# A transformer-like layer on one core: the down product of its channel mixer as seven half-size products

## The chip, the core and the metric

One core of a Trainium2 chip runs the whole program. TensorE multiplies, VectorE (DVE in the profile), ScalarE (ACT) and GpSimd (POOL) do the elementwise work, SyncE (SP) issues the transfers. The metric is the device time of one execution in microseconds; the median of three runs of the kernel before is 1348.81 us (1346.97 to 1351.1).

## The reference, cut to what matters

One layer of a streaming encoder over 592 tokens (16 meta, 512 prompt, 64 sample): a differential attention and a gated delta rule side by side, merged, and then the channel mixer, which works on the 576 tokens whose result is given back:

```python
x = x + mix @ p["w_out"]
h2 = _rmsnorm(x, p["norm2"])
x = x + jnp.square(jax.nn.relu(h2 @ p["w_up"])) @ p["w_down"]
```

`w_up` is 1024 x 4096, `w_down` 4096 x 1024, all in 32-bit floats. The change lies in the last line.

## The kernel before, in words

Every product is made of three: each operand is split into a high part (rounded to the type that TensorE multiplies in one pass, by a copy on ScalarE) and a low part (what is left, by a subtraction on DVE or GpSimd), and high x high, high x low and low x high are added up in PSUM. Tokens lie along the free axis, in two halves of 288.

`stream` (line 292) runs a list of tasks, one for each 256 columns of a weight matrix. While the body of task i issues matmuls, it hands out small steps at each `yield`, from the body's second on: the high part of the next weights' first 512 rows (`split_hi`, 128 x 1024 elements), their low part (`split_lo`), the same for the other 512 rows, and the loads for the task after next into the two buffers `wr0` and `wr4` (tiles `wr_*`, 512 KB each). High and low parts are the tiles `wh_*` and `wl_*`, two buffers each. `VG` (line 281) chooses DVE or GpSimd for a low part by the clocks that the planner `Pace` (line 52) keeps for each engine.

`feat` (line 362) is the body of most tasks: four parts (two blocks of 128 output features x two halves of tokens), each of 8 blocks of 128 input features x 3 matmuls, 24 in all, into one PSUM bank; it yields after every eight. The bank's evacuation `evac` is issued when its last matmul has been. Three banks go round (tag `pg`); the other five (tag `pt`) serve everything else.

The channel mixer: `up_task(i)` (line 1405), sixteen of them, each for 256 of the 4096 hidden features. Its evacuation of one part reads PSUM with relu and the norm's scale (DVE, tile `ur`), squares (ScalarE), and splits into `uh` (copy on ScalarE) and `ul` (subtraction on DVE). `down_tasks(qd)` (line 1421) are four tasks for each quarter of the hidden features; each multiplies 1024 hidden features into 256 outputs and adds the PSUM result to the running sum `x1` (DVE, tile `x`). The order is written out at line 1468: up 0 to 4, down 0, up 5 to 8, down 1, up 9 to 12, down 2, up 13 to 15, down 3. In the last quarter `write_y` (line 1437) turns each finished pair of blocks of `x1` and stores it.

Ahead of the mixer, `norm2_part` (line 1358) splits `x1` times the norm's weight into `h2h` and `h2l` and adds up squares; `token_norm` (line 1378) makes the reciprocal root for each token and spreads it over the partitions as `rstd2`, by a product of ones with five scaled identities `dg`. The up product starts on the unscaled values; only its evacuation needs `rstd2`.

Engines run their instructions in the order in which the program issues them, and wait on semaphores for each other. `Chain` objects (attention, norm, output) are woven in by `drive` (line 341).

Of the kernel before, what the change touches and what calls it, by code (L numbers as in the profile page):

```python
# [8 lines left out]
F32 = mybir.dt.float32  # L9
F32R = mybir.dt.float32r  # L10
# [7 lines left out]
P = 128  # L18
# [12 lines left out]
QHALVES = ((0, 288), (288, 576))  # L31
QTILES = [(0, 128), (128, 128), (256, 128), (384, 128), (512, 64)]
# [167 lines left out]
class Task:  # L200


    def __init__(self, nm, src, c0, body, need=None):
        self.nm, self.src, self.c0, self.body = nm, src, c0, body
        self.need = need or (lambda: True)


@with_exitstack
def stream_step_kernel(
# [24 lines left out]
    gp = Tags(pace, ctx.enter_context(pool("gates")), gth=3, st=3)  # L234
# [57 lines left out]
    def stream(tasks):  # L292
        raw, wts = {}, {}

        def load(i, k):
            if i < len(tasks) and tasks[i].src is not None:
                t = tasks[i]

                def go():
                    raw[i, k] = wp.tile([P, 4, 256], F32, name=f"wr_{t.nm}{k}", tag=f"wr{k}")  # L300
                    Q.dma_start(raw[i, k], t.src[k * P:(k + 4) * P, t.c0:t.c0 + 256].rearrange("(k p) n -> p k n", p=P))
                pace.stores.append((wp.when(f"wr{k}", 1), ((i, k),), go))
                if "start" not in done:
                    pace.flush(key=(i, k))

        def split_hi(i, k):
            pace.flush(key=(i, k))
            if (i, k) in raw:
                if k == 0:
                    wts[i] = [wp.tile([P, KC, 256], F32R, name=f"{x}_{tasks[i].nm}", tag=x) for x in ("wh", "wl")]  # L310
                S.copy(wts[i][0][:, k:k + 4], raw[i, k])

        def split_lo(i, k):
            if (i, k) in raw:
                hi, lo = (x[:, k:k + 4] for x in wts[i])
                (VG(2.1, 1024) if "start" in done else G).tensor_tensor(lo, raw.pop((i, k)), hi.bitcast(F32), ALU.subtract)

        for k in (0, 4):
            load(0, k)
        yield False  # L320
        for k in (0, 4):
            split_hi(0, k)
            split_lo(0, k)
        yield False
        for k in (0, 4):
            load(1, k)
        for i, t in enumerate(tasks):
            while not t.need():
                yield False
            ahead = deque()  # L330
            for f, j, k in ((split_hi, 1, 0), (split_lo, 1, 0), (split_hi, 1, 4), (load, 2, 0), (split_lo, 1, 4),
                            (split_lo, 1, 8), (load, 2, 4)):
                ahead.append(lambda f=f, j=j, k=k: f(i + j, k))
            for n, x in enumerate(t.body(wts.pop(i, None))):
                if n >= 1 and ahead and "start" in done and x is None:
                    ahead.popleft()()
                yield x is None
            while ahead:
                ahead.popleft()()
# [21 lines left out]

    def feat(xh, xl, nm, evac, m=P, ms=(0, P), halves=QHALVES, after="start", last=None):

        def body(w):
            parts, full = [(h, c) for h in range(len(ms)) for c in halves], deque()
# [23 lines left out]

    def tok(xh, xl, nm, evac):  # L390
# [16 lines left out]
    cst = cp.tile([P, 3 * P], F32, name="cst")  # L407
    ident = cst[:, 0:128]
    UP = (cst[:, 128:256], cst[:, 256:384])
    identr = cp.tile([P, P], F32R, name="identr")  # L410
    onesr = cp.tile([P, P], F32R, name="onesr")
    lowr = cp.tile([P, 2, P], F32R, name="lowr")
    nmr = cp.tile([P, 2, P], F32R, name="nmr")
    kn_bc = cp.tile([P, 64], F32, name="kn_bc")
# [3 lines left out]
    vec2 = cp.tile([P, 75], F32, name="vec2")  # L418
# [7 lines left out]
    g_t = cp.tile([P, NT, 8], F32, name="g_t")  # L426
    beta_t = cp.tile([P, NT, 8], F32, name="beta_t")
    gh_t = cp.tile([P, NT, 8], F32R, name="gh_t")
    gl_t = cp.tile([P, NT, 8], F32R, name="gl_t")
    kdec = cp.tile([P, NT, 8], F32, name="kdec")  # L430
    egl = cp.tile([P, NT + 1, 8], F32, name="egl")
    rn = cp.tile([P, 4, 2, NT, 4], F32, name="rn")
    cs_t = cp.tile([P, 2, 72], F32, name="cs_t")
# [32 lines left out]
    def begin(sp):  # L466
# [20 lines left out]
        Q.dma_start(cst[:, P:3 * P], consts[:, P:3 * P])  # L487
# [63 lines left out]
    def prepare(sp):  # L551
# [15 lines left out]
        V.tensor_scalar(nmr, cst[:, P:3 * P].rearrange("p (a b) -> p a b", a=2), -MASKED, MASKED, ALU.mult, ALU.add)  # L567
# [468 lines left out]
    def attn_tasks(p):  # L1036
        def evac(i):
            def f(t, n, ps):
                x = gp.tile([P, 256], F32, name=f"st{p}{i}{t}", tag="st")
# [3 lines left out]
                if i < 2:  # L1043
                    jk = gp.tile([P, 256], F32, name=f"sq{p}{i}{t}", tag="sq")
# [4 lines left out]
                if t == NT - 1:  # L1049
                    if i == 1:  # L1050
                        r = rn[:, p].rearrange("t i a m -> t (i a m)")
                        rsqrt(gp, r, 40, 1.0 / 64, EPS, tag="ar", out=r)
# [305 lines left out]
    def norm2_part(j):  # L1358
# [6 lines left out]
        if j == 0:  # L1365
            late["sq"] = rp.tile([P, TQ], F32, name="sqa", tag="sqa")
# [198 lines left out]
```

## Time and profile before

| | us |
|---|---|
| median of three runs | 1348.81 |
| profiled execution | 1348.32 |
| its span, first to last instruction | 1346.5 |
| TensorE matmul busy | 1297.8 |
| DVE busy | 694.0 |
| ScalarE busy | 564.5 |
| GpSimd busy | 264.7 |
| chain: four up tasks (384 matmuls) | 50.92 |
| chain: four down tasks (384 matmuls) | 50.97 |

Busy times are sums over instructions, in the profile as shares of the span. Matmuls are pipelined: each is printed with some 0.295 us though the next starts 0.13 us later, so times of TensorE are best read from starts. The same holds in small for the other engines: an instruction can start some 0.08 us ahead of the printed end of the one before. The chain of waits is followed back from the last instruction; its rows give a start, a length, an engine and a tile.

### The profile page before, as it was taken

The numbers are of one execution on the slowest core, as the hardware profiler recorded it, in microseconds if no ns is written. First come the engines' busy times: TensorE is split into PE (matmuls) and PEld (weight loads), VectorE is DVE, ScalarE is ACT, GpSimd is POOL, SyncE is SP. The second block draws the span as 40 slices with busy tenths as digits, with TensorE's granted clock in tenths as the row PEclk, the third lists the DMA queues.
The fourth block names the chain that finished last, engine by engine and source line by source line (L and its number), as shares of the span: only waits on it lengthen the run. The fifth ranks groups of instructions, "written<-read, shape, count | busy, mean of one in ns | idle before, by whom it ended". The sixth has DMA issues, their size and how long they took to land.

```text
span 1346.5 us, 25748 instructions
## 1 busy us (share of the span) xinstructions
PE 1297.8 (96%) x10365; PEld 1260.4 (94%) x10365; DVE 694.0 (52%) x1547; ACT 564.5 (42%) x1354; POOL 264.7 (20%) x283
## 2 busy tenths in 40 slices
PE   2999999999999999999899999999999999999998
PEld 2998899999899999998788899999999999999998
DVE  5766899533457624448877844445333233233232
ACT  3556544343563343346676723233431431431421
POOL 5101412200132000062524102100410410310300
PEclk9999999999999999999999899999999999999999
DMA  6313343532644422685644256622223223222231
GB/s 174 90 53 116 100 124 113 169 91 72 196 135 127 141 78 66 189 242 162 198 141 135 94 203 226 204 78 80 79 79 95 76 82 94 67 92 86 72 112 53
DMA packets 163947, 161.07 MB, mean 120 GB/s; under 512 B 23546, under 2 KB 143628, under 8 KB 163828
## 3 DMA queue, kind: packets, MB, share of 16 engines
q1 hardware_dynamic: 162372, 155.99, 38.2%
q0 software_dynamic: 1456, 3.44, 0.9%
q8 instruction: 81, 1.33, 0.4%
q14 instruction: 38, 0.31, 0.1%
HBM read 124.46 MB, written 37.88 MB: 121 GB/s over the span
## 4 chain that ended last, share of the span: by engine, by line
PE 46%; DVE 3%; DMA 1%; ACT 1%; issue 0%; SPq 0%; DVEq 0%; ACTq 0%
PE pg_dn L164 15%; PE pg_u L164 15%; PE pg_o L164 4%; PE pg_bb L164 4%; PE pg_ba L164 3%; PE pg_g L164 1%; DVE sc L164 1%; PE ppo L164 1%; DVE mx L164 1%; PE psc L164 1%; PE pwT L164 1%; ACT sc L164 0%; DMA thb<-th_d 0%; PE pxr L164 0%; PE pyo L164 0%
## 5 line engine op out<-in xcount | busy, mean ns | idle before, releaser
L164 PE MATMUL pg_dn<-uh,wh_dn 128*128 128x288 f32 x512 | 151.6, 296 | 0.0
L164 PE MATMUL pg_dn<-ul,wh_dn 128*128 128x288 f32 x512 | 151.6, 296 | 0.0
L164 PE MATMUL pg_u<-h2h,wh_u 128*128 128x288 f32 x512 | 151.4, 296 | 0.0
L164 PE MATMUL pg_u<-h2h,wl_u 128*128 128x288 f32 x512 | 151.2, 295 | 0.0
L164 PE MATMUL pg_u<-h2l,wh_u 128*128 128x288 f32 x512 | 151.2, 295 | 0.0
L164 PE MATMUL pg_dn<-uh,wl_dn 128*128 128x288 f32 x512 | 151.1, 295 | 0.0
L164 PE MATMUL pg_a<-wh_a,hh 128*128 128x256 f32 (+1 forms) x480 | 136.3, 284 | 2.0 <-ACT sq L164 2.0
L164 PE MATMUL pg_a<-wh_a,hl 128*128 128x256 f32 (+1 forms) x480 | 136.3, 284 | 0.0
L164 PE MATMUL pg_a<-wl_a,hh 128*128 128x256 f32 (+1 forms) x480 | 135.4, 282 | 0.0
L164 PE MATMUL pg_d<-hl,wh_d 128*128 128x336 f32 (+1 forms) x384 | 116.1, 302 | 0.6 <-DVE hl L164 0.6
L164 PE MATMUL pg_d<-hh,wh_d 128*128 128x336 f32 (+1 forms) x384 | 116.0, 302 | 0.6 <-ACT hh L164 0.6
L164 PE MATMUL pg_d<-hh,wl_d 128*128 128x336 f32 (+1 forms) x384 | 115.8, 302 | 0.0
L164 POOL TENSOR_TENSOR wl_u<-wr_u,wh_u 128x1024 fp32r<-128x1024 f32 x22 | 52.9, 2402 | 260.5 <-ACT wh_u L164 260.5
L164 DVE TENSOR_TENSOR x<-x,pg_dn 128x288 f32<-128x288 f32 x64 | 29.1, 454 | 132.5 <-PE pg_dn L164 132.5
L164 PEld LDWEIGHTS pg_u<-h2h,wh_u 128*128 128x128 f32 x512 | 96.5, 189 | 0.1
L164 PEld LDWEIGHTS pg_u<-h2l,wh_u 128*128 128x128 f32 x512 | 96.5, 189 | 0.0
L164 PEld LDWEIGHTS pg_u<-h2h,wl_u 128*128 128x128 f32 x512 | 96.4, 188 | 0.0
L164 PEld LDWEIGHTS pg_dn<-uh,wl_dn 128*128 128x128 f32 x512 | 96.3, 188 | 0.0
L164 PEld LDWEIGHTS pg_dn<-ul,wh_dn 128*128 128x128 f32 x512 | 96.1, 188 | 0.0
L164 PEld LDWEIGHTS pg_dn<-uh,wh_dn 128*128 128x128 f32 x512 | 96.1, 188 | 0.0
L164 PEld LDWEIGHTS pg_a<-wh_a,hh 128*128 128x128 f32 (+1 forms) x480 | 86.5, 180 | 3.1 <-ACT sq L164 2.5
L164 PEld LDWEIGHTS pg_a<-wh_a,hl 128*128 128x128 f32 (+1 forms) x480 | 86.7, 181 | 0.7 <-issue 0.6
(371 smaller groups left out, 3536.6 us busy)
## 6 DMA issues: line engine op xcount, KB each, us to landing
wr_u<-in_w_up_dram SPq DMA_DIRECT2D x32, 512.0 KB, 3.6
wr_dn<-in_w_down_dram SPq DMA_DIRECT2D x32, 512.0 KB, 3.5
wr_d<-in_w_in_dram SPq DMA_DIRECT2D x24, 512.0 KB, 3.9
wr_a<-in_w_in_dram SPq DMA_DIRECT2D x24, 512.0 KB, 4.1
wr_g<-in_w_in_dram SPq DMA_DIRECT2D x16, 512.0 KB, 5.5
at_d<-st SPq DMA_DIRECT2D x48, 128.0 KB, 2.2
th_d<-gt SPq DMA_DIRECT2D x16, 288.0 KB, 2.2
wr_z<-in_w_in_dram SPq DMA_DIRECT2D x8, 512.0 KB, 3.8
```

The costliest lines, as they stand in the source:

```text
L164: r = f(*a, **kw)
```

## The change

A down task takes four blocks of its factors as a 2 x 2 matrix: the weights as rows (even and odd blocks of 128 hidden features) by columns (two blocks of 128 outputs), the hidden values as rows by columns (two halves of tokens). Seven products of half the size replace the eight, after the scheme of Strassen and Winograd. Each is of 4 blocks of hidden features x 3 matmuls of 128 x 128 x 288.

The sums of the weights are made by four DVE steps (`s1` to `s4`, 128 x 512 elements each, partly in place); high and low parts are then made of 3.5 x 1024 elements in place of 2 x 1024, in two blocks of buffers, the second within the task itself. The seven combinations of hidden values are made by the up tasks' evacuation: a tile of seven for each up task, with four differences. Of the up task's two token halves, the second block of features takes the later one first (`turn`). The seven products go into four PSUM banks; three go on in a bank after DVE has read it. P1 and P6 are added into a tile `G` of their own over the four quarters, and `G` is added to three of the four result blocks in the last quarter. The first down task of the last quarter issues its products in the order `LATE`. The low parts of weights stay off GpSimd from the out product on (`VG` then gives DVE). Constants of the early stages move to a pool that is closed before the mixer, to make room; the weight loads have a third buffer `wrx`; `token_norm` multiplies with the reciprocal root spread by a stride of zero instead of the scaled identities; the squares go to `rstd2` and the `gth` buffers.

```diff
@@ VG
+        if "tail" in done:
+            return V
         return V if max(pace.t["DVE"], pace.t["PE"]) + 1.05 * n <= ...
@@ stream
+        users = {"wr0": deque(), "wr4": deque(), "wrx": deque()}
...
+        def room():
+            return len([x for x in held if not x["free"]]) < 2
...
+        def plain_steps(i):
...
+            return [(room, lambda: hi(0)), (None, lambda: lo(0)), (None, lambda: hi(1)), (None, lambda: load("wr0")),
+                    (None, lambda: lo(1)), (None, lambda: load("wr4"))]
...
+        def seven_steps(i):
...
+            def s1():
+                (_, a21), (_, a22) = quarters(0), quarters(1)
+                st["s"] = late["wx"].tile([P, 4, 256], F32, name=f"s_{tasks[i].nm}", tag="ws")
+                VG(2.1, 512).tensor_tensor(st["s"][:, :, 0:128], a21, a22, ALU.add)
+            def s2():
+                VG(2.1, 512).tensor_tensor(st["s"][:, :, 128:256], st["s"][:, :, 0:128], quarters(0)[0], ALU.subtract)
+            def s3():
+                a11, a21 = quarters(0)
+                VG(2.1, 512).tensor_tensor(a21, a11, a21, ALU.subtract)
+            def s4():
+                a12 = quarters(1)[0]
+                VG(2.1, 512).tensor_tensor(a12, a12, st["s"][:, :, 128:256], ALU.subtract)
...
+            before = [(None, s1), (None, s2), (None, s3),
+                      (room, lambda: hi(0, 0, r0)), (None, lambda: lo(0, 0, r0, tag="wr0")),
+                      (None, lambda: hi(0, 1, s)), (None, lambda: lo(0, 1, s))]
+            own = [(room, lambda: hi(1, 0, r1)), (None, lambda: lo(1, 0, r1)), (None, s4),
+                   (None, lambda: hi(1, 1, r1, 128)), (None, lambda: lo(1, 1, r1, 128, tag=odd_tag[i]))]
...
+            ahead = deque(own.pop(i, []))
+            ahead.extend(before(i + 1))
...
+                if n >= (0 if t.seven else 1) and ahead and "start" in done and x is None:
+                    if ahead[0][0] is None or ahead[0][0]():
+                        ahead.popleft()[1]()
@@ seven: the body of a down task (block of weights, its quarter, combination, bank)
+    SEVEN = {1: (0, 0, 0, "a"), 6: (0, 3, 6, "b"), 7: (0, 1, 3, "c"), 5: (0, 2, 4, "d"),
+             2: (1, 0, 1, "a"), 4: (1, 1, 5, "c"), 3: (1, 2, 2, "d")}
+    EVEN = [(p, range(4)) for p in SEVEN]
+    LATE = [(p, range(3)) for p in (1, 6, 7, 5)] + [(p, range(3, 4)) for p in (1, 6, 7, 5)] + [(p, range(4)) for p in (2, 4, 3)]
...
+                    for i, (ww, xx) in enumerate(((wh, xh), (wh, xl), (wl, xh))):
+                        TE.matmul(ps[bk], ww, xx, start=p in (1, 6, 7, 5) and k == 0 and i == 0, stop=k == 3 and i == 2,
+                                  skip_group_check=True)
+                        n += 1
+                        if k == 3 and i == 2:
+                            w[0]["free"] = p in (5, 2, 4, 3)
...
+                            evac(p, ps[bk])
+                        elif n < 6:
+                            continue
+                        n = 0
+                        yield
@@ up_task
-            S.activation(r[:, a:b], r[:, a:b], AF.Square)
-            split(uh[j][:, a:b], ul[j][:, a:b], r[:, a:b])
+        def part(dst, src, n):
+            S.copy(us[i][0][:, dst:dst + n], src)
+            V.tensor_tensor(us[i][1][:, dst:dst + n], src, us[i][0][:, dst:dst + n].bitcast(F32), ALU.subtract)
...
+            k = 2 * h + (a > 0) if h else int(a == 0)
+            V.scalar_tensor_tensor(r[:, k], ps, 0.0, late["rstd2"][:, a:b], ALU.max, ALU.mult)
+            S.activation(r[:, k], r[:, k], AF.Square)
+            if k == 1:
+                part(0, r[:, 1:2], 1)
+            elif k == 0:
+                V.tensor_tensor(r[:, 1], r[:, 0], r[:, 1], ALU.subtract)
+                part(4, r[:, 1:2], 1)
+            elif k == 3:
+                part(2, r[:, 3:4], 1)
+                V.tensor_tensor(r[:, 0], r[:, 3], r[:, 0], ALU.subtract)
+                V.tensor_tensor(r[:, 3], r[:, 3], r[:, 1], ALU.subtract)
+                part(3, r[:, 0:1], 1)
+                part(6, r[:, 3:4], 1)
+            else:
+                part(1, r[:, 2:3], 1)
+                V.tensor_tensor(r[:, 2], r[:, 2], r[:, 3], ALU.subtract)
+                part(5, r[:, 2:3], 1)
+                done.add(f"u{i}")
@@ down_tasks
-                V.tensor_tensor(x1[:, j, a:b], x1[:, j, a:b], ps, ALU.add)
...
+                if p == 1 and qd == 0:
+                    S.copy(g, ps)
+                    return
+                x = {1: g, 6: g, 7: x22, 5: x22, 2: x11, 4: x21, 3: x12}[p]
+                V.tensor_tensor(x, x, ps, ALU.add)
+                if qd == 3 and p == 6:
+                    x2 = x1[:, 2 * c + 1].rearrange("p (a b) -> p a b", a=2)
+                    VG(2.1, TQ).tensor_tensor(x2, x2, g[:, None, :].to_broadcast([P, 2, TH]), ALU.add)
+                    VG(2.1, TH).tensor_tensor(x12, x12, g, ALU.add)
@@ token_norm
-                dg = rp.tile([P, P], F32, name=f"dg{t}", tag="dg")
-                V.tensor_scalar(dg[:n, :n], ident[:n, :n], r[:n, t:t + 1], None, ALU.mult)
-                TE.matmul(ps[:, c0 - b0:c0 - b0 + n], onesr[:n, :].bitcast(F32), dg[:n, :n], start=True, stop=True)
+                TE.matmul(ps[:, c0 - b0:c0 - b0 + n], r[:n, t:t + 1].to_broadcast([n, P]), ident[:n, :n], start=True, stop=True)
```

## Rows read from the trace of the kernel before

**Rows 1.** The page, part 1: busy us (share of the span) xinstructions.
```profile
PE 1297.8 (96%) x10365; PEld 1260.4 (94%) x10365; DVE 694.0 (52%) x1547; ACT 564.5 (42%) x1354; POOL 264.7 (20%) x283
```
**Rows 2.** The chain of waits in the channel mixer: start, us, engine, tile.
```profile
1044.37 50.92 PE pg_u L164 x384
1095.28 50.97 PE pg_dn L164 x384
1248.14 38.18 PE pg_u L164 x288
```
**Rows 3.** Groups of instructions from 926.7 us on: busy us, mean ns, idle before.
```profile
L164 POOL TENSOR_TENSOR wl_u<-wr_u,wh_u 128x1024 fp32r<-128x1024 f32 x22 | 52.9, 2402 | 260.5 <-ACT wh_u L164 260.5
...
L164 DVE TENSOR_TENSOR ul<-ur,uh 128x288 fp32r<-128x288 f32 x64 | 31.5, 492 | 62.5 <-ACT uh L164 62.5
L164 DVE SCALAR_TENSOR_TENSOR ur<-pg_u,rstd 128x288 f32<-128x288 f32 x64 | 29.3, 458 | 81.5 <-PE pg_u L164 80.3 <-ACT rstd L164 1.2
L164 DVE TENSOR_TENSOR wl_dn<-wr_dn,wh_dn 128x1024 fp32r<-128x1024 f32 x24 | 29.3, 1219 | 0.0
L164 DVE TENSOR_TENSOR x<-x,pg_dn 128x288 f32<-128x288 f32 x64 | 29.1, 454 | 132.5 <-PE pg_dn L164 132.5
```
**Rows 4.** Timeline of DVE in four stretches: start, us, instruction, [idle before <-releaser].
```profile
882.47 1.22 DVE L164 TENSOR_TENSOR wl_o<-wr_o,wh_o 128x1024 fp32r<-128x1024 f32 x1
883.60 0.81 DVE L164 SCALAR_TENSOR_TENSOR h2l<-x,vec,h2h 128x576 fp32r<-128x576 f32 x1
...
936.21 0.46 DVE L164 SCALAR_TENSOR_TENSOR ur<-pg_u,rstd 128x288 f32<-128x288 f32 x1 [1.18 <-ACT rstd L164]
937.64 0.46 DVE L164 TENSOR_TENSOR ul<-ur,uh 128x288 fp32r<-128x288 f32 x1 [0.97 <-ACT uh L164]
938.02 0.45 DVE L164 SCALAR_TENSOR_TENSOR ur<-pg_u,rstd 128x288 f32<-128x288 f32 x1
...
1060.28 0.46 DVE L164 SCALAR_TENSOR_TENSOR ur<-pg_u,rstd 128x288 f32<-128x288 f32 x1 [1.27 <-PE pg_u L164]
1061.72 0.61 DVE L164 TENSOR_TENSOR ul<-ur,uh 128x288 fp32r<-128x288 f32 x1 [0.98 <-ACT uh L164]
...
1098.49 0.45 DVE L164 TENSOR_TENSOR x<-x,pg_dn 128x288 f32<-128x288 f32 x1 [1.28 <-PE pg_dn L164]
1098.87 1.22 DVE L164 TENSOR_TENSOR wl_dn<-wr_dn,wh_dn 128x1024 fp32r<-128x1024 f32 x1
```
**Rows 5.** Timeline of ScalarE in the evacuation that DVE began at 1060.28.
```profile
1060.78 0.45 ACT L164 ACTIVATE ur<-ur 128x288 f32<-128x288 f32 x1 [1.30 <-DVE ur L164]
1061.25 0.44 ACT L164 CAST uh<-ur 128x288 fp32r<-128x288 f32 x1
1061.59 1.04 ACT L164 CAST wh_u<-wr_u 128x1024 fp32r<-128x1024 f32 x1
```
**Rows 6.** Groups of instructions up to 926 us: one of 512 elements on DVE.
```profile
L164 DVE TENSOR_TENSOR ktok<-ktok,kdec 128x512 f32<-128x512 f32 x5 | 3.4, 684 | 0.0
```
**Rows 7.** Who waited for whom: TensorE in the norm (us, times, longest).
```profile
PE prs L164 <- DVE dg L164: 0.2, 1, 0.2
```
**Rows 8.** DMA issues of the down weights: KB each, median us to landing.
```profile
wr_dn<-in_w_down_dram SPq DMA_DIRECT2D x32, 512.0 KB, 3.5
```
**Rows 9.** Stretches around two gaps of TensorE: busy us of each engine, granted clock, DMA.
```profile
142.00:145.20 3.20, 0.72 (x6) 0.44 (x4) 3.20 (x6) 1.60 (x4) 2.44 (x6) 1.00 0.29 52
145.20:150.20 5.00, 5.00 (x32) 4.97 (x33) 3.17 (x5) 2.81 (x6) 0.00 (x0) 0.66 0.19 64
352.50:354.00 1.50, 0.05 (x2) 0.05 (x1) 1.39 (x5) 0.00 (x0) 0.00 (x0) 1.00 1.09 376
354.00:359.00 5.00, 5.00 (x45) 5.00 (x46) 1.64 (x3) 1.59 (x3) 0.00 (x0) 1.00 0.95 300
```
**Rows 10.** Timeline of TensorE in a stretch of half clock.
```profile
748.95 0.44 PE L164 MATMUL pg_bb<-hh,wh_bb 128*128 128x288 f32 x1
749.19 0.44 PE L164 MATMUL pg_bb<-hl,wh_bb 128*128 128x288 f32 x1
```

More of the change, by code (lines that the diff above doesn't have):

```diff
@@ L292, in stream @@
     def stream(tasks):
[L293 to L304, printed above, removed]
@@ L306, in split_hi @@
-        def split_hi(i, k):
-            pace.flush(key=(i, k))
-            if (i, k) in raw:
-                if k == 0:
[L310 to L316, printed above, removed]
@@ L318, in stream @@
-        for k in (0, 4):
-            load(0, k)
-        yield False
-        for k in (0, 4):
-            split_hi(0, k)
-            split_lo(0, k)
+        raw, wts, held = {}, {}, []
+        users = {"wr0": deque(), "wr4": deque(), "wrx": deque()}
+        for i, t in enumerate(tasks):
+            if t.src is not None:
+                odd = "wr4" if not t.seven or sum(x.seven for x in tasks[:i]) % 2 else "wrx"
+                users["wr0"].append((i, 0, "wr0"))
+                users[odd].append((i, 1, odd))
@@ new lines, in stream, with load, go @@
+        odd_tag = {i: tag for q in ("wr4", "wrx") for i, _, tag in users[q]}
+        def load(tag):
+            if not users[tag]:
+                return
+            i, k, _ = users[tag].popleft()
+            t = tasks[i]
+            pl = late["wx"] if tag == "wrx" else wp
+            def go():
+                raw[i, k] = pl.tile([P, 4, 256], F32, name=f"wr_{t.nm}{k}", tag=tag)
+                src = t.src[:, t.c0:t.c0 + 256]
+                if t.seven:
+                    src = src.rearrange("(k t p) n -> t p k n", t=2, p=P)[k]
+                else:
+                    src = src[4 * k * P:(4 * k + 4) * P].rearrange("(k p) n -> p k n", p=P)
+                Q.dma_start(raw[i, k], src)
+            pace.stores.append((pl.when(tag, 1), ((i, k),), go))
+            if "start" not in done:
+                pace.flush(key=(i, k))
+            if k == 0 and odd_tag[i] == "wrx" and "wx1" not in done:
+                done.add("wx1")
+                load("wrx")
@@ L324, in stream, with before @@
+        for tag in ("wr0", "wr4"):
+            load(tag)
+        yield False
+        own = {}
+        def before(i):
+            if i >= len(tasks) or tasks[i].src is None:
+                return []
+            if not tasks[i].seven:
+                return plain_steps(i)
+            b, own[i] = seven_steps(i)
+            return b
+        first = before(0)
+        for k in (0, 1, 2, 4):
+            first[k][1]()
         yield False
-        for k in (0, 4):
-            load(1, k)
+        for k in (3, 5):
+            first[k][1]()
@@ L360, in drive, with feat @@
         pace.flush()
-    def feat(xh, xl, nm, evac, m=P, ms=(0, P), halves=QHALVES, after="start", last=None):
+    def feat(xh, xl, nm, evac, m=P, ms=(0, P), halves=QHALVES, after="start", last=None, turn=False):
         def body(w):
-            parts, full = [(h, c) for h in range(len(ms)) for c in halves], deque()
+            parts, full = [(h, c) for h in range(len(ms)) for c in (halves[::-1] if turn and h else halves)], deque()
             if "start" not in done:
@@ L1417, in body @@
         def body(w):
-            yield from feat(late["h2h"], late["h2l"], f"u{i}", evac, after="mlp")(w)
+            yield from feat(late["h2h"], late["h2l"], f"u{i}", evac, after="mlp", turn=True)(w)
+            if i == 15:
+                done.add("up")
         return Task(f"u{i}", w_up[0], i * 256, body, has("h2") if i == 0 else None)
@@ L1440, in write_y @@
         yield
+        while "y" not in late:
+            yield
         for t, (c0, n) in enumerate(QTILES):
```

175 lines of the change are left out of this document (117 added, 58 removed).

## The prediction, made before the change was run

> **What bounds the kernel now.** I read the page's busy shares first, then the chain that ended last, then the grouped lines of the channel mixer, and last the timelines of the vector engines. TensorE is busy for 96% of the span [rows 1]. From the out product to the end the chain is TensorE alone: 384 matmuls of four up tasks take 50.92 us and 384 of four down tasks 50.97 us, one after the other [rows 2]. That is 0.1327 us from one 288-column matmul to the next, 12.74 us for a task of 96. The others are far below that: of the DVE work in this stretch, the PSUM reads of the up product make 29.3 us, the low parts 31.5 us, the PSUM adds of the down product 29.1 us and the weights' low parts 29.3 us, and GpSimd does 22 of the low parts of the up weights [rows 3]. So a matmul that goes is worth its full 0.1327 us, as long as nothing else becomes late.
>
> **What the change removes from the path.** Each of 16 down tasks has 7 products of 4 x 3 matmuls in place of 8: 84 instead of 96, of the same shape (288 columns, 128x128 weights). 16 x 12 = 192 matmuls, 192 x 0.1327 = 25.5 us. A down task then takes 11.15 us.
>
> **What it puts on DVE, in lengths.** DVE's step from one start to the next is shorter than the printed duration: 0.38 us for 288 elements (1098.49 to 1098.87), 1.13 us for 1024 (882.47 to 883.60) [rows 4]. 512 elements print 0.684 us [rows 6], so I take 0.60. Down task: four sums of 512 (2.40), low parts of 3 x 1024 + 512 (3.99), seven PSUM reads (2.66): 9.05 us beside 11.15 us of TensorE. In the last quarter two more adds (576 and 288 elements, about 1.2 us) and three copies of y. ScalarE and SyncE have room: a weight load lands 3.5 us after issue [rows 8] and its buffer is free some 7 us ahead of its use. Up task: four PSUM reads, four differences, seven low parts, 15 x 0.38 = 5.7, and both low parts of the next weights, which GpSimd mostly did, 2.26: 7.96 us of 12.74. By lengths alone all of it is hidden and the time is 1348.3 - 25.5 = 1323.
>
> **What it puts on DVE, in waits.** DVE runs its queue in the order written, and one evacuation is a chain with ScalarE. Before: read at 1060.28, ScalarE's square at 1060.78, its copy at 1061.25, DVE's low part at 1061.72 [rows 4, 5]. So DVE to ScalarE is 0.50 us, ScalarE to ScalarE 0.47, ScalarE to DVE 0.47. With the results already waiting, one such evacuation holds DVE for 1.81 us (936.21 to 938.02) [rows 4], though it works for 0.76. After the change, with the same steps:
> first quarter: read, square, copy, low part: 1.82.
> second: read, square (0.50), difference (0.97), copy (1.47), low part (1.94): 2.32.
> third: low part of r at 1.44, two differences at 1.82 and 2.20, copies at 2.32 and 2.70, low parts at 2.79 and 3.17: 3.55.
> fourth: low part at 1.44, difference 1.82, copy 2.32, low part 2.79: 3.17.
> Sum 10.86, with the next weights' low parts 13.12 us. TensorE's task is 12.74. DVE therefore falls behind by 0.38 us in each up task, where it had 3 us to spare (4 x 1.81 + 2.26 = 9.5).
> TensorE doesn't notice this within the up tasks: three PSUM banks let a read be 6.4 us late. It notices at the first down task. The last up task of a block carries three sums and two low parts (4.06 instead of 2.26), and ScalarE's copy of the sums is queued ahead of a square (0.55). From the third quarter of the block's first task on DVE never catches up; the four tasks' last evacuations end 16.6, 29.7, 42.8 and 58.3 us after the block began, and the down task begins at 50.96: it is e = 7.3 us late.
>
> **What is queued behind it.** In the first down task the fifth product (P2) needs DVE's read of P1, whose bank it goes on with, and the low part of the second weight block, for which ScalarE's copy (1.04 us) comes after that last evacuation's: it is done at e + 0.56, the low part (1.22) at e + 1.85. Without lateness it would be wanted at 6.64. Then P4 waits for the read of P7 (behind a sum, a read and a low part, e + 4.22), P3 for the read of P5 (e + 6.28), and the next task's P1 for a low part that waits for ScalarE's copy, which waits for the third sum (e + 9.2). The next task so begins at e + 8.9 instead of 11.15: a block loses e - 2.2 = 5.1 us. From there on the down tasks hold: each has some 0.8 us of margin at its tightest point. Blocks one to three: 5.2 + 5.1 + 5.1 (the first starts late, since the norm before it holds back three parts, but the weights' low parts are done by then). The last block has three up tasks (e = 7.0), and its order takes the P1 read after the first sum of the next task and the two large adds ahead of P7's: P2 at e + 4.8, P4 at e + 8.1, end at e + 11.3, 7.1 us lost. Together 22.5.
> By the Trainium skill (TensorE: Matmul & The Clock Gate, the section on the array of 16 sub-arrays) ScalarE and VectorE are strict FIFO queues, while TensorE can pull weight loads ahead. By that rule nothing behind a waiting low part can pass it, and the sum has its 22.5 us; were it not so, the 1323 above would stand. The trace agrees in so far as DVE stood 0.98 us ahead of each low part [rows 4], but no row shows ready work behind it there.
>
> **Smaller terms.** The norm's five scaled identities go; TensorE waited 0.2 us for them [rows 7]: -0.2. The square sums move to DVE in the out product, where it has half of its time free: 0. Slower low parts beside GpSimd (0.492 us on the mean against 0.458 for the read [rows 3]) go: inside the 0.38 used. Loads are issued a step earlier in the tasks before: 0, with +-2 us since an order of emission shifts. TensorE's clock: after a stretch of 3.2 us in which it worked for 0.72 us its granted clock was 0.66 over the next 5 us, that is 1.2 GHz for part of them; after 1.5 us with 0.05 us of work it stayed at 1.00, 2.4 GHz [rows 9]. At 1.2 GHz matmuls start 0.24 us apart [rows 10]. P2's stall of about 2.5 us lies between those rows, so a drop is likely; at 0.34 x 5 us / 0.5 = 3.4 us of half clock it costs 3.4 x (1 - 0.1327/0.24) = 1.5 us. In the first three blocks P4's wait hides most of it; in the last nothing does. I take 0.1 + 0.1 + 0.1 + 1.5 = 1.8; bounds 0 and 6.
>
> **Sum.** -25.5 + 22.5 + 1.8 - 0.2 = -1.4 us on the profiled 1348.3 (span 1346.5 and 1.8 around it): 1346.9. The median of the runs shown is 1348.8, half a microsecond above the profiled one. A measurement of this kernel tells about 0.3% (4 us) from no change, so this is no change.
>
> **Rivals.**
> 1. The gain is half kept (1338). If an evacuation holds DVE some 0.1 us less than summed, 13.12 falls to 12.74 and the lateness doesn't add up over the block; e is then 5.4, a block loses 3.2, the last 5.5: 15 us, -25.5 + 15 = -10. For it: the margin is 3%. Against: the back-to-back row gives 1.81 where I sum 1.82.
> 2. All of it is kept (1323): DVE's waits are covered after all, as by lengths. Against: 0.98 us of idle time ahead of each low part, with the same order as after.
> 3. Slower (1360). An up task has 16 handovers between DVE and ScalarE in a row. If each is 0.05 us dearer than in the rows (instructions that wait for two engines, weight copies in between), DVE needs 13.9 us a task, e grows by 3.2, four blocks lose 12.8 us more; with the clock falling in each, +12. It turns slower from about 0.02 us for each handover on. For it: the chains are longer than any that the trace shows; against: the two kinds of handover are measured on the same shapes.
> 4. TensorE's matmuls don't shrink by 192, because the split isn't as said: 1349 or more. The diff's table has seven entries of 4 x 3, so hardly.
>
> **Chances and range.** Forecast (within 4 us of no change) 0.40, its own range 1341 to 1353; rival 1 0.31; rival 2 0.05; rival 3 0.22; rival 4 0.02, which goes with no change or slower. Faster by over 0.3%: 0.36; within: 0.41; slower: 0.23. Range 1335 to 1360: it leaves out rival 2 and the far part of rival 3.
>
> **What would show it.** 84 matmuls in a down task, about 0.133 us apart, and no work on GpSimd after the out product. In the up stretches TensorE without gaps, DVE over 95% occupied or waiting for ScalarE, and reads of PSUM starting later from part to part. A gap of TensorE ahead of P2 of tasks 00, 10, 20, 30 (2 to 3 us, in the last 5), then about 1 us ahead of P4 and of the next task's first product, and none in the three tasks that follow. Four down tasks in 49 to 51 us instead of 50.97. Wrong if four down tasks take 45 us (rival 2), or if TensorE is also held up within the up tasks or in every down task (rival 3).

## The result, and the profile after

The changed kernel is slower: 1370.29 us (median of 4 runs, 1366.55 to 1374.07) against 1347.89 us for the kernel before beside it (4 runs, 1344.41 to 1351.1). The ratio is 1.0174 with a 95% interval of 1.015 to 1.0198, so 22.4 us are lost. The profiled execution took 1366.55 us, with a span of 1364.6. The prediction was 1346.9, its range 1335 to 1360.

The page of the kernel after, part 1, answers to [rows 1]: TensorE has exactly the 192 matmuls less that the change promises, DVE works 171 us more, and GpSimd 78 us less.

```profile
PE 1291.3 (95%) x10173; PEld 1250.0 (92%) x10173; DVE 864.6 (63%) x1836; ACT 613.2 (45%) x1438; POOL 186.3 (14%) x249
```

Where the 22 us went is not to be seen in busy shares. I cut the span at the first matmul of one stage and the next. The views that give these times are the answers for one tile: operation, count, minimum, median and maximum of its duration in ns, then the first and the last start in us. First the kernel before (gate product and up product):

```profile
L164 PE MATMUL pg_g<-hh,wh_g x256: 289/296/404, 426.9 to 743.7; 128*128 128x288 f32 x128
...
L164 PE MATMUL pg_u<-h2h,wh_u x512: 293/296/402, 926.5 to 1285.8; 128*128 128x288 f32 x171
```

And the same tiles in the kernel after:

```profile
L165 PE MATMUL pg_g<-hh,wh_g x256: 290/297/442, 422.6 to 740.7; 128*128 128x288 f32 x128
...
L165 PE MATMUL pg_u<-h2h,wh_u x512: 293/296/400, 942.8 to 1301.5; 128*128 128x288 f32 x171
```

The chain of waits of the kernel after gives the later cuts (start, us, engine, tile); its rows answer to [rows 2]. It now leaves TensorE after 48 matmuls of a block of up tasks and runs through DVE and ScalarE, which is the first sign that DVE has become late.

```profile
1061.08 6.41 PE pg_u L165 x48
...
1162.37 6.41 PE pg_u L165 x48
...
1263.67 6.41 PE pg_u L165 x48
```

| stretch | before | after | change | predicted |
|---|---|---|---|---|
| start to the gate product | 426.9 | 422.6 | -4.3 | 0 |
| gate product to up product | 499.6 | 520.2 | **+20.6** | **0** |
| five up tasks, four down tasks | 117.9 | 118.3 | +0.4 | -1.3 |
| two rounds of four up and four down tasks | 203.8 | 202.6 | -1.2 | -2.3 |
| three up tasks, four down tasks, end | 98.4 | 100.9 | +2.5 | +2.2 |

The first line is one execution against another: over the profiles of the two kernels and of ten experiments below, in which the order of instructions up to the gate product is the same, that product begins anywhere from 422.6 to 428.4 us. So two facts are left. The channel mixer, where nearly all the work of the change lies, costs 1.8 us more (421.8 against 420.0). And 20.6 us are lost ahead of it, in a stretch whose arithmetic the diff doesn't touch.

Who kept TensorE waiting in the kernel after, by the view of waits (us in total, times, longest):

```profile
...
PE pxr L165 <- DMA x_r<-in_x_prompt_dram: 7.2, 1, 7.2
PE pa_dn L165 <- DVE G L165: 5.9, 1, 5.9
PE pwT L165 <- DVE sc L165: 5.8, 3, 4.5
...
PE pa_dn L165 <- ACT wh_dn L165: 3.9, 2, 1.9
PE pg_bb L165 <- ACT hh L165: 2.9, 1, 2.9
PE pa_dn L165 <- DVE wl_dn L165: 2.8, 4, 0.7
PE pa_dn L165 <- ACT G L165: 2.4, 1, 2.4
```

The rows with `dn` are the mixer's. The others lie between 590 and 945 us, in attention (`pwT`), branch B (`pg_bb`) and the residual's transposes (`pxr`). There the gaps of at least 0.8 us sum up to 21.6 us, where the kernel before has 10.0. The rest of the 20.6 is lower clock and shorter gaps: TensorE's granted clock is 0.96 on the mean from 590 us to the up product, where it was 0.99. The windows around the two longest gaps (columns as in [rows 9]) show it:

```profile
645.00:653.00 8.00, 3.54 (x28) 3.31 (x27) 7.58 (x15) 3.81 (x10) 6.22 (x9) 0.85 0.18 56
653.00:660.00 7.00, 7.00 (x40) 6.56 (x41) 4.91 (x12) 2.92 (x8) 0.00 (x0) 0.68 0.56 182
825.40:833.50 8.10, 0.93 (x7) 0.79 (x5) 2.15 (x4) 1.23 (x3) 0.00 (x0) 0.67 0.64 214
833.50:843.00 9.50, 9.50 (x56) 9.27 (x55) 2.71 (x4) 4.82 (x7) 3.06 (x2) 0.74 0.47 152
```

The last gap, 7.2 us, is a transpose that waits for the residual's load. Its place in SyncE's queue is behind loads of the attention's result, which follow the store of that result's last part:

```profile
803.71 0.32 SPq L165 DMA_DIRECT2D oa_d<-oaT  x1
804.12 0.38 SPq L165 DMA_DIRECT2D oa<-oa_d  x1
...
828.63 0.42 SPq L165 DMA_DIRECT2D x_r<-in_x_prompt_dram  x1
```

The same two in the kernel before:

```profile
788.51 0.32 SPq L164 DMA_DIRECT2D oa_d<-oaT  x1
...
821.67 0.42 SPq L164 DMA_DIRECT2D x_r<-in_x_prompt_dram  x1
```

So attention ends some 15 us later, and what hangs on it moves with it.

### The profile page after: what moved, and what is told of

Its sections match the earlier page's. It is cut to its first block, busy times and chain, and to the rows that moved or that the text cites. A ratio compares the mean times of both kernels' runs of the same rounds, so it can differ in the third digit from the quotient of the medians.

```text
span 1364.6 us, 25675 instructions
## 1 busy us (share of the span) xinstructions
PE 1291.3 (95%) x10173; PEld 1250.0 (92%) x10173; DVE 864.6 (63%) x1836; ACT 613.2 (45%) x1438; POOL 186.3 (14%) x249
## 4 chain that ended last, share of the span: by engine, by line
PE 68%; DVE 15%; ACT 9%; DMA 4%; issue 3%; SPq 1%; POOL 0%; DVEq 0%; ACTq 0%; POOLq 0%
PE pg_a L165 10%; PE pg_d L165 9%; PE pg_g L165 7%; PE pg_ba L165 4%; PE pg_z L165 4%; PE pg_o L165 4%; DVE r L165 3%; PE pa_dn L165 3%; PE pc_dn L165 3%; PE pd_dn L165 3%; ACT uh L165 3%; DVE ul L165 3%; PE pg_bb L165 2%; ACT r L165 2%; PE ppo L165 2%
## 5 line engine op out<-in xcount | busy, mean ns | idle before, releaser
L165 DVE TENSOR_TENSOR ul<-r,uh 128x288 fp32r<-128x288 f32 x112 | 51.3, 458 | 63.5 <-ACT uh L165 62.8
L165 ACT CAST wh_dn<-wr_dn 128x1024 fp32r<-128x1024 f32 (+1 forms) x48 | 43.5, 906 | 98.1 <-DVE wr_dn L165 87.2
L165 PEld LDWEIGHTS pg_a<-wl_a,hh 128*128 128x128 f32 (+1 forms) x480 | 86.5, 180 | 0.3 <-issue 0.2
L165 PE MATMUL pg_g<-hh,wl_g 128*128 128x288 f32 x256 | 78.6, 307 | 0.0
L165 PE MATMUL pg_g<-hl,wh_g 128*128 128x288 f32 x256 | 78.2, 305 | 0.0
L165 PE MATMUL pg_g<-hh,wh_g 128*128 128x288 f32 x256 | 78.2, 305 | 0.0
L165 PEld LDWEIGHTS pg_d<-hl,wh_d 128*128 128x128 f32 x384 | 72.4, 189 | 1.8 <-DVE hl L165 1.1
L165 PEld LDWEIGHTS pg_d<-hh,wh_d 128*128 128x128 f32 x384 | 72.4, 189 | 1.3 <-ACT hh L165 1.2
```

The lines of the kernel that those rows point to most:

```text
L165: r = f(*a, **kw)
```

## The experiments

Two questions were open: what moved the attention, and what would be left of the change without DVE's lateness.

### Which part of the diff loses the time ahead of the mixer

**The changed kernel with the steps of the tasks ahead of the out product handed out as before.** The old list had seven steps, of which the sixth, `(split_lo, 1, 8)`, issues nothing; the new one has six, and the tail of the list moves up by one. The instructions ahead of the out product then have the order of the kernel before.

```diff
+            if "tail" in done:
...
+            nop = lambda: None
...
+            return [(room, lambda: hi(0)), (None, lambda: lo(0)), (None, lambda: hi(1)),
+                    (None, (lambda: load("wr0")) if nxt else nop), (None, lambda: lo(1)), (None, nop),
+                    (None, (lambda: load("wr4")) if nxt else nop)]
```

> The changed kernel with the list of steps ahead of the out product as it was before (the empty seventh step back in, the loads around the task ba one task later), nothing else. Theory A, order: the 16 us that the changed kernel is late at the start of the up product (942.98 against 926.67 us) come from the order that the planner writes once a step is gone; the up product then starts at about 927 us, the mixer takes 421.6 us as in the changed kernel, 1348 to 1353 us in all. Rival M, memory: the new places of the merge's and the mixer's tiles make them wait for older ones; it stays at 1366 to 1374 us.

Measured: 1349.52 us (10 runs), ratio to the kernel before 0.9998 (0.9977 to 1.0019). The up product begins at 926.8 us, and from there to the end it takes 421.7. In its trace every engine runs its instructions up to the out product in the order of the kernel before. So the mixer alone is no change, which is what the prediction said of it, and the whole loss is the order of steps.

**The kernel before without its empty step**, nothing of the seven products:

```diff
             for f, j, k in ((split_hi, 1, 0), (split_lo, 1, 0), (split_hi, 1, 4), (load, 2, 0), (split_lo, 1, 4),
-                            (split_lo, 1, 8), (load, 2, 4)):
+                            (load, 2, 4)):
```

> The kernel before without the empty step (split_lo, 1, 8) of its list, nothing else; the eight-product mixer and the old places of all tiles stay. Theory A, order: the up product starts some 16 us later, 1362 to 1367 us in all, ratio 1.010 to 1.014. Rival M, memory: 1348 us, ratio 0.998 to 1.002.

Measured: 1371.3 us (4 runs), ratio 1.0173 (1.0137 to 1.0209). One step that issues no instruction is worth the full 1.7%, more than the 1.0 to 1.4% that I had expected. Up to the out product its trace has the instructions in the order of the kernel after, on every engine. Its profile repeats the waits of the kernel after, first the load of the residual, then attention's:

```profile
PE pxr L164 <- DMA x_r<-in_x_prompt_dram: 7.5, 1, 7.5
PE pwT L164 <- DVE sc L164: 6.4, 3, 5.0
```

**The empty step gone from one task only.** Read off the program, of the tasks 17 to 51 only two change the order of TensorE's instructions when the step goes from them alone: 33 (the first task of gate A) and 37 (the first of branch B). Three more (26, 36 and 38) only let a few transfers or splits change places; the expectation takes them for unchanged, and they were not run by themselves.

```diff
-                ahead.append(lambda f=f, j=j, k=k: f(i + j, k))
+                if not (i == 33 and k == 8):
+                    ahead.append(lambda f=f, j=j, k=k: f(i + j, k))
```

> The kernel before with the empty step gone in one task only, number 33 of the list (the first of the four tasks of gate A, which run beside the attention). Leaving it out in any one of the tasks 17 to 32, 34 to 36 or 38 to 51 gives the same order of instructions as before; 33 and 37 are the two that count. Theory: this one step moves one weight load ahead of a head's loads in the planner's books, the turns of that head go one or two places back, and the attention ends some 15 us later: 1362 to 1373 us, most of what e2 lost. Rival: the loss is shared among many small shifts, the branch product's tasks as well: 1350 to 1358 us.

> As g33_one_task, with the empty step gone in task 37 only (the first of branch B). Theory: the attention up to the fifth or sixth head keeps its order, so that its end is at most a few us later: 1346 to 1356 us. Rival: here lies the loss: 1362 to 1373 us.

Measured: 1370.86 us for task 33 (4 runs), ratio 1.0193 (1.0157 to 1.0229); 1352.32 for task 37 (7 runs), ratio 1.0054 (1.0035 to 1.0073). Task 33 alone costs the whole loss. In the timeline of SyncE's queue the place can be seen. The kernel before:

```profile
631.17 0.75 SPq L164 DMA_DIRECT2D ma<-ob_d  x1
632.01 0.41 SPq L164 DMA_DIRECT2D mb<-z_d  x1
632.52 0.39 SPq L164 DMA_DIRECT2D wr_g<-in_w_in_dram  x1
```

And without the empty step in task 33:

```profile
632.52 0.84 SPq L164 DMA_DIRECT2D wr_g<-in_w_in_dram  x1
633.42 0.52 SPq L164 DMA_DIRECT2D ma<-ob_d  x1
633.99 0.42 SPq L164 DMA_DIRECT2D mb<-z_d  x1
```

One load of 512 KB goes ahead of one pair of loads of the delta rule's output. That is less than I had expected here, where I put loads of an attention head behind it. From there on the planner meets other clocks and weaves the attention's and the delta rule's instructions in another order; the last store of the attention's result is issued at 812.46 us, not at 788.51. Which of the planner's comparisons tips first was not traced.

**Two empty steps, and the empty step one place earlier**, both in the kernel before:

```diff
-                            (split_lo, 1, 8), (load, 2, 4)):
+                            (split_lo, 1, 8), (split_lo, 1, 8), (load, 2, 4)):
```

```diff
-            for f, j, k in ((split_hi, 1, 0), (split_lo, 1, 0), (split_hi, 1, 4), (load, 2, 0), (split_lo, 1, 4),
-                            (split_lo, 1, 8), (load, 2, 4)):
+            for f, j, k in ((split_hi, 1, 0), (split_lo, 1, 0), (split_hi, 1, 4), (load, 2, 0), (split_lo, 1, 8),
+                            (split_lo, 1, 4), (load, 2, 4)):
```

> The kernel before with two empty steps in a row in place of one; nothing that runs is added or taken. Theory, order as a draw: the planner's order changes from the early tasks on, and the time moves by several us either way, 1340 to 1372 us, not tied to the number of steps. Rival, lateness: one step less issues the loads earlier and costs 22 us, so one step more issues them later and is neutral or a little better, 1340 to 1350 us.

> The kernel before with the empty step one place earlier, ahead of the second low part instead of behind it: the low part comes one turn later, the loads where they were. Theory, order as a draw: a different order from the delta rule on, 1345 to 1375 us, with no rule which. Rival: only loads that come earlier cost, so here the time stays within 1345 to 1351 us.

Measured: 1357.12 us (9 runs), ratio 1.0055 (1.003 to 1.008), and 1365.69 (4 runs), ratio 1.0153 (1.0121 to 1.0185). Later loads lose a little too, and a low part that is one step late loses most of what the earlier loads lost. So this is no cost of one direction, such as earlier loads: the kernel before happens to have a good order, and every shift that was tried was slower.

**Is it the late load of the residual?** The kernel before without the empty step, with the planner told to use the first part of the residual 10 us later:

```diff
-            yield pace.free(xt) + 4000
+            yield pace.free(xt) + (14000 if t == 0 else 4000)
```

> e2_no_empty_step (eight products, empty step gone) with one number changed: the planner thinks that the first block of the residual is ready 14 us after its buffer is free instead of 4, so that its turns stand later in TensorE's queue. Theory: the longest early wait, 7.5 us ahead of the first turn of the residual, is there because the turn stands ahead of matmuls that could run; with its clock drop it is worth 8 to 11 us: 1360 to 1364 us, ratio about 1.010. Rival: the load is simply late and the next turn or the branch product waits in its place: 1368 to 1374 us.

Measured: 1370.68 us (4 runs), ratio 1.0172 (1.0151 to 1.0193): nothing gained. The wait of 7.5 us is gone from TensorE's waits, and branch A's wait for the attention's result stands in its place:

```profile
PE pwT L164 <- DVE sc L164: 7.2, 4, 5.0
PE pg_ba L164 <- ACT oh L164: 6.5, 2, 4.7
```

So the longest wait in the list was not the cause, and the residual only happened to be first in line. What fits every run is the end of attention: in all fourteen profiles the up product begins 135 to 143 us after the last store of the attention's result, be that store issued at 786 us or at 813. That this end sets the rest is argued from there; no run moved it alone.

### What DVE's lateness in the mixer costs

**The low parts of the up tasks one evacuation later**, on top of the old steps. DVE no longer stands still until ScalarE has made the high part: it first reads the next PSUM bank, and then does the low parts of the evacuation before. Two differences go to other slots of `r`, so that none is overwritten while a low part still needs it.

```diff
-        def part(dst, src, n):
+        def part(dst, src):
-            S.copy(us[i][0][:, dst:dst + n], src)
-            V.tensor_tensor(us[i][1][:, dst:dst + n], src, us[i][0][:, dst:dst + n].bitcast(F32), ALU.subtract)
+            S.copy(us[i][0][:, dst:dst + 1], src)
+            lows.append(lambda: V.tensor_tensor(us[i][1][:, dst:dst + 1], src, us[i][0][:, dst:dst + 1].bitcast(F32), ALU.subtract))
...
             S.activation(r[:, k], r[:, k], AF.Square)
+            while lows:
+                lows.popleft()()
```

> e1_old_steps, and in the up tasks' evacuation DVE does the low parts of a part only after it has read the next one (two differences get another place so that their sources stay). The same instructions in number and length. Theory W, waits: DVE loses 27 us of the mixer's gain to waits for ScalarE; without them the first three blocks lose nothing, the last about 3 us and a clock drop: the mixer takes 397 to 402 us, 1324 to 1331 us in all. Rival L, lengths: DVE is simply too full with 8 to 9 us of work in tasks of 11 to 13 us; as in e1_old_steps, 1348 to 1353 us.

Measured: 1327.97 us (1325.92 to 1329.4, 4 runs), ratio 0.9858 (0.9831 to 0.9885). The mixer takes 400.4 us (926.6 to 1327.0), 21.3 less than with the low parts where the change has them. The groups of the mixer answer to [rows 3] (busy us, mean ns, idle just before and who ended it). First the kernel after:

```profile
L165 DVE TENSOR_TENSOR ul<-r,uh 128x288 fp32r<-128x288 f32 x112 | 51.3, 458 | 63.5 <-ACT uh L165 62.8
...
L165 DVE SCALAR_TENSOR_TENSOR r<-pg_u,rstd 128x288 f32<-128x288 f32 x64 | 28.9, 451 | 10.2 <-PE pg_u L165 8.4 <-ACT rstd L165 1.7
```

Then this kernel:

```profile
L165 DVE TENSOR_TENSOR ul<-r,uh 128x288 fp32r<-128x288 f32 x112 | 46.5, 449 | 0.7 <-ACT uh L165 0.6
...
L165 DVE SCALAR_TENSOR_TENSOR r<-pg_u,rstd 128x288 f32<-128x288 f32 x64 | 29.2, 457 | 61.5 <-PE pg_u L165 59.8 <-ACT rstd L165 1.7
```

The idle time hasn't gone; it has changed its place. In the kernel after DVE spent 62.8 us in front of low parts, with the next PSUM result mostly waiting already (only 8.4 us of waiting for TensorE, where [rows 3] has 80.3). Here it spends the same time waiting for TensorE, which is where an engine off the path should wait. In the up tasks the chain is TensorE's alone again:

```profile
1038.56 51.20 PE pg_u L165 x384
...
1135.00 51.21 PE pg_u L165 x384
...
1231.43 38.41 PE pg_u L165 x288
```

A round of four up and four down tasks is 96.4 us (1038.56 to 1135.00), where it was 101.9 [rows 2].

**The changed kernel itself with late low parts**, the same edit without the old steps, to see whether the two effects add up:

```diff
-            V.tensor_tensor(us[i][1][:, dst:dst + n], src, us[i][0][:, dst:dst + n].bitcast(F32), ALU.subtract)
+            lows.append(lambda: V.tensor_tensor(us[i][1][:, dst:dst + 1], src, us[i][0][:, dst:dst + 1].bitcast(F32), ALU.subtract))
...
+            while lows:
+                lows.popleft()()
```

> The changed kernel as it is, early order included, with the late low parts of e3_late_lows in the up tasks alone. Theory: the two losses are apart. The mixer gains the 21.5 us that it gained in e3 against e1 (1327.97 against 1349.52), the early order keeps its 16 to 22 us: 1346 to 1352 us, ratio 0.998 to 1.003. Rival: part of the early loss is owed to the mixer's tiles and goes with it, or the two overlap: under 1342 us.

Measured: 1350.49 us (10 runs), ratio 1.0023 (1.0004 to 1.0041), 19.8 us below the median of the kernel after. Where the low parts stand and how the steps ahead of the mixer are ordered are two separate costs of about 20 us each.

**Is there more to have?** The late low parts with the sums of `G` into the result after P5 in place of P6, and without a step in the place where one stood ahead of a read in the first task of the last quarter:

```diff
-                if n >= (0 if t.seven else 1) and ahead and "start" in done and x is None:
+                if n >= (0 if t.seven else 1) and not (t.nm == "dn30" and n == 5) and ahead and "start" in done and x is None:
...
-                if qd == 3 and p == 6:
+                if qd == 3 and p == 5:
```

> e3_late_lows, and in the first task of the last quarter the sum for the next task isn't made ahead of P1's read; in the whole last quarter the two adds of G come after P5's read instead of P6's. Theory, in-order DVE: the two waits that e3 has left there (1.49 us for P1's read, 1.18 us for P7's) go: 1.5 to 2.7 us less than e3, 1325 to 1327 us. Rival: DVE is full there and the wait moves to P3 or to the next task: as e3, 1328 us.

Measured: 1327.89 us (4 runs), ratio 0.9853 (0.9834 to 0.9872). The wait for `G` fell from 1.5 to 0.9 us, and the time stayed where it was, within what can be measured.

### Whether GpSimd could have helped

**GpSimd allowed in the mixer again**, once with the order of the change (old steps ahead of the mixer) and once with late low parts; the rule of `VG` for the stretch from the out product on is left out in both:

```diff
-        if "tail" in done:
-            return V
```

> e1_old_steps without the rule that keeps weights' low parts and sums off GpSimd in the mixer; the planner chooses again and gives GpSimd most low parts of the up weights and about half the sums. The chains with ScalarE stay. Theory W, waits: DVE's up task falls from 13.1 to about 10.9 us, it no longer gets late from task to task, and the first down tasks lose 3.2 us instead of 5 to 7: some 8 to 10 us less than e1_old_steps, 1339 to 1345 us, as long as a 2.4 us step on GpSimd isn't itself late. Rival L, lengths: the full gain, 1325 to 1330 us.

> e3_late_lows without the rule that keeps GpSimd out of the mixer (as e4 against e1). Theory from e4's trace: TensorE waited there for low parts from GpSimd (2.4 us each) at the second block of weights and DVE's reads were later, not earlier; with DVE's waits for ScalarE gone DVE has room, so GpSimd's share can only be late: 1334 to 1348 us. Rival, e4's loss came from the chains with ScalarE being slowed by the shared work: with the chains gone GpSimd costs nothing, 1326 to 1330 us.

Measured: 1365.24 us (4 runs), ratio 1.0135 (1.011 to 1.0161), and 1335.77 (5 runs), ratio 0.9931 (0.9907 to 0.9955). Both are slower than the same kernel without GpSimd, by 15.7 us in the medians of one round, and by 7.8 us in the medians of two rounds (9.7 in the mixer's stretch, 410.1 against 400.4). Both numbers expected of the first miss it. The groups say why. With the order of the change:

```profile
L165 DVE TENSOR_TENSOR ul<-r,uh 128x288 fp32r<-128x288 f32 x112 | 65.8, 587 | 63.7 <-ACT uh L165 62.8
...
L165 POOL TENSOR_TENSOR wl_u<-wr_u,wh_u 128x1024 fp32r<-128x1024 f32 x20 | 48.9, 2461 | 180.9 <-ACT wh_u L165 180.9
...
L165 DVE TENSOR_TENSOR x<-x,G 128x576 f32<-128x576 f32 x3 | 4.2, 1388 | 0.1
```

With late low parts:

```profile
L165 DVE TENSOR_TENSOR ul<-r,uh 128x288 fp32r<-128x288 f32 x112 | 96.2, 893 | 1.8 <-ACT uh L165 0.6
```

The same low part of 288 elements takes 458 ns on the mean with the order of the change and 449 with late low parts when GpSimd stays out, 587 and 893 with it. These means mix two kinds: with late low parts and GpSimd, 82 of the 112 met no GpSimd instruction and took 0.45 us on the mean, and the 30 that did took 2.10, each of them ending 0.31 to 0.33 us behind the end of a GpSimd instruction. One such pair, from the timelines of GpSimd and DVE:

```profile
1044.53 2.39 POOL L165 TENSOR_TENSOR wl_u<-wr_u,wh_u 128x1024 fp32r<-128x1024 f32 x1 [0.77 <-ACT wh_u L165]
1045.67 1.56 DVE L165 TENSOR_TENSOR ul<-r,uh 128x288 fp32r<-128x288 f32 x1
```

What GpSimd takes over is given back by DVE's slower instructions: from the up product to the end GpSimd is busy for 142.6 and 134.5 us in the two kernels, and DVE's busy time only goes from 300.0 to 289.5 and from 293.4 to 294.0 us. With the order of the change TensorE also waited 8.2 us for low parts that GpSimd made. "No GpSimd there" is a part of the change that earns its place.

## Why the prediction was wrong, point by point

**The step that failed** is in the smaller terms: "Loads are issued a step earlier in the tasks before: 0, with +-2 us since an order of emission shifts." It measured 20.6 us in the profiled execution, and 23 us in medians with that one edit alone. I priced the loads, which indeed have room, and not the planner, which weaves attention and delta rule around them by its clocks. The bound of 2 us had no row behind it: none of the rows of before shows the kernel with another order. No rival covered it, so the range ended at 1360.

**The mixer, where the working went,** came out at +1.8 us, predicted -1.4. Its steps:

*192 matmuls less, 25.5 us.* Right: 10365 to 10173, and with the late low parts 19.6 us of it reach the end (the mixer takes 400.4 us, where the kernel before takes 420.0).

*An evacuation is a chain with ScalarE, and DVE needs 13.12 us a task where TensorE needs 12.74.* Right. In DVE's timeline of the kernel after (start, us, instruction, idle before) four parts, from the third of one up task to the third of the next, go from 1084.19 to 1097.43, 13.24 us, in parts of 3.62, 3.26, 1.80 and 2.30 us and two low parts of weights of 1.13. I had summed 3.55, 3.17, 1.82, 2.32 and the same:

```profile
1084.19 0.45 DVE L165 SCALAR_TENSOR_TENSOR r<-pg_u,rstd 128x288 f32<-128x288 f32 x1
1085.61 0.46 DVE L165 TENSOR_TENSOR ul<-r,uh 128x288 fp32r<-128x288 f32 x1 [0.97 <-ACT uh L165]
...
1087.81 0.45 DVE L165 SCALAR_TENSOR_TENSOR r<-pg_u,rstd 128x288 f32<-128x288 f32 x1
...
1091.07 0.45 DVE L165 SCALAR_TENSOR_TENSOR r<-pg_u,rstd 128x288 f32<-128x288 f32 x1
...
1092.87 1.22 DVE L165 TENSOR_TENSOR wl_u<-wr_u,wh_u 128x1024 fp32r<-128x1024 f32 x1
1094.00 0.45 DVE L165 SCALAR_TENSOR_TENSOR r<-pg_u,rstd 128x288 f32<-128x288 f32 x1
...
1096.30 1.22 DVE L165 TENSOR_TENSOR wl_u<-wr_u,wh_u 128x1024 fp32r<-128x1024 f32 x1
1097.43 0.45 DVE L165 SCALAR_TENSOR_TENSOR r<-pg_u,rstd 128x288 f32<-128x288 f32 x1
```

The reads come without any idle time before them: the PSUM result lies there, and DVE is the late one. In [rows 4] such a read waited 1.27 us for TensorE.

*The lateness at the first down task, e = 7.3.* It is 8.0: the block's last low part is done at 1119.97, four up tasks of 12.73 us after 1061.08 is 1112.0. The four parts run over or under by 0.1 us or less, 0.12 in a task, which adds up over four; the square that ScalarE does behind the copy of the sums holds DVE for 1.14 us, where an ordinary one holds it for 0.51, about the 0.55 more that I had put there.

*The stalls ahead of P2, 2 to 3 us and 5 in the last block.* Right within 1 us: 2.36, 1.93, 1.94 and 5.89 us. *About 1 us more ahead of P4 and the next task's first product.* Mostly not there: 0.45 and 0.62 us, once each. With three waits of 0.73 us ahead of a matmul that needs a low part of the weights, all waits of the mixer from 0.4 us up sum to 15.4 us, where I had 22.5. The four down tasks of the second block took 50.4 us (1112.0 to 1162.37), within the 49 to 51 expected.

*The clock, 1.8 us.* Too small, and this fills most of the hole. In each block, at the stall ahead of P2 or soon behind it, the matmuls begin to stand 0.24 us apart for a while (1.2 GHz), here after the first stall (timeline of TensorE, as in [rows 10]):

```profile
1019.37 0.61 PE L165 MATMUL pa_dn<-uh,wh_dn 128*128 128x288 f32 x1 [2.36 <-ACT G L165]
...
1020.74 0.44 PE L165 MATMUL pa_dn<-uh,wh_dn 128*128 128x288 f32 x1
1020.98 0.44 PE L165 MATMUL pa_dn<-ul,wh_dn 128*128 128x288 f32 x1
...
1025.61 0.44 PE L165 MATMUL pc_dn<-uh,wl_dn 128*128 128x288 f32 x1
```

Counted over the four blocks, 70 to 75 matmuls go at this pitch (25 in the first), 0.107 us dearer each: some 8 us. I expected the drop and its size in one place, but let P4's wait hide it in three of the four blocks. By the sums it is the other way round: the slow matmuls take the time in which P4 would have waited. Waits and clock together are some 23.4 us, predicted 24.3; what was given back is 25.5 + 1.8 = 27.3. Some 4 us lie in gaps below 0.4 us and in slower starts behind a wait, and were not separated. That the two errors nearly cancel is in part luck; that a stall's clock and the next wait are one budget is what was missed, though no run tests it alone.

*By the Trainium skill* (TensorE: Matmul & The Clock Gate, the section on the array of 16 sub-arrays) VectorE's queue is strictly first in, first out. By that rule no PSUM read that was ready could pass a low part that waited for ScalarE. The runs agree: with instructions of the same number and length in another order on DVE, the median falls by 21.5 us.

*Slower low parts beside GpSimd.* The sign was right and the size was not asked for: with GpSimd back the mixer loses 16 us.

**The rivals.** The first (1338, half kept) asked for 0.1 us less in an evacuation than summed; the parts measured have no such margin. The third (1360, slower) named the right side for the wrong reason: its mark, TensorE held up within the up tasks, isn't there: in the window from 1061 to 1112 it works without a gap at full clock.

```profile
1061.00:1112.00 51.00, 51.00 (x385) 51.00 (x384) 31.83 (x63) 23.78 (x45) 0.00 (x0) 1.00 0.25 77
```

The second, 1323, is what the order of DVE withheld: 1328 was reached with late low parts. The fourth fell with the count of matmuls.

## What to carry to other kernels

Where a planner orders the work by clocks, a change to its list of steps can reorder everything behind it, even a step that issues nothing; run the order alone first, with the old arithmetic, and price it by that run. Where two engines hand parts of one evacuation back and forth in order, issue the dependent step after the next independent one: the idle time then falls where nobody waits for it. And when the longest wait in the list is taken away and the time doesn't move, go up the chain to what ended late.

## What the runs showed of the hardware that I had not expected

- TensorE's granted clock fell at a stall of 2.36 us in the middle of a stretch that was busy otherwise (mean 0.50 from 1019.4 to 1024.4 us). The 25 matmuls behind it went at the pitch of 1.2 GHz; the up tasks just after have 1.00. With the stalls of 1.93 and 1.94 us it stayed at 1.00 for the first 1.0 us behind them, and fell during or behind a second wait, of 0.7 us, that began some 0.5 us after the stall. Yet a gap of 2.97 us in attention, ended at 727.6 in the kernel after, and one of 2.12, ended at 670.2 in the kernel before, left it at 1.00 for the 5 us that followed. So the length of a gap alone doesn't tell.
- DVE's subtraction of two operands in SBUF slows down beside GpSimd's of the same kind by far more than the kernel before let see: 0.492 us on the mean there [rows 3], 0.587 and 0.893 in the two kernels above, and 1.39 us in place of 0.758 for 576 elements. GpSimd's own went from 2.40 us [rows 3] to 2.46. A rule of the Trainium skill (SBUF — State Buffer, the section on the two separate sides) says that a DVE instruction with two inputs in SBUF and a GpSimd instruction that reads SBUF take a shared pair of ports for the whole instruction, and the one that comes second waits. The trace agrees: the 30 low parts that met GpSimd ended 0.31 to 0.33 us behind it. In the kernel before 27 of the 64 did so too, but they began so near GpSimd's end that none took more than 0.61 us.
- Between executions of the same instructions the gate product began up to 5.8 us earlier or later, so a span alone can hide or feign a few microseconds. Cutting it at stages helps where the order holds: from the gate product to the up product the order of the kernel before took 499.6 to 501.5 us in six profiles, but that of the kernel after 520.2 to 525.9 in three.
